# Where in a partition the MLP's stationary operands begin: two tiles allocated ahead of the weight buffers, and operand sets 32 bytes further on

## The chip, the cores and the metric

The kernel runs on one core of a Trainium2 chip. The metric is device time in microseconds (us); lower is better. Three runs of the kernel before took 2269.15, 2271.0 and 2269.58 us, median 2269.58.

## The reference

One step of a decoder layer for 320 token rows (256 prompt rows, 8 x 8 sample rows) of width 2048, in float32. Only the outline matters here:

```python
proj   = x @ w_in                                 # 2048 -> 16392 columns, split among all heads and gates
a      = mLSTM(q, k, v, gates, state)             # 4 heads, 256 x 512 matrix memory
b      = HGRN2(q, f, i, state)                    # 8 heads, 128 x 256 state
merged = sigmoid(gate_a) * (a @ w_branch_a) + sigmoid(gate_b) * (b @ w_branch_b)
x1     = layernorm(alpha * x + merged @ w_out)
hid    = square(relu(x1 @ w_up))                  # 2048 -> 8192
y      = layernorm(alpha * x1 + hid @ w_down)     # 8192 -> 2048
# y and the new states of both mixers are the outputs
```

## The kernel before

Every large product is made of float32r matmuls. A float32 operand is split into a high half (a rounded copy, made by ScalarE, ACT) and a low half (the rest, a subtraction on VectorE, DVE), and one product is the sum of three matmuls: high x high, low x high, high x low. A matmul has a stationary operand, 128 x 128, that a weight load (PEld in the profile) brings into the array, and a moving operand that streams through it. Each matmul here has its own weight load, which runs beside the matmul ahead of it. In a profile row `bank<-A,B` the names are those of the two operands in alphabetical order; with 320 columns the weights are stationary and the activations move, with 512 columns it is the other way round (below).

The phases, with their place in the profiled span:

- 0 to about 900 us: the input projection, with the two mixers' own small matmuls between. Stationary are slices of the weight halves `wh` and `wl`, moving are the 320 columns of `xh` and `xl`.
- about 900 to 1370 us: output gates, both branch projections and `w_out`, again with weights stationary (in `wh`, `wl`, and from here on in parts of `bb` as well) and 320 moving columns from `xh`, `xl`, `rxh`, `ra` and `bb`.
- about 1370 to 2236 us: the MLP, in 8 parts (`PH`) of 1024 hidden columns. The up-projection goes on with 320 moving columns. The down-projection turns the roles: stationary are 128 x 128 pieces of the hidden activations, moving are 512 columns of `w_down` (halves in `wh`, `wl` and parts of `bb`). In parts 0 to 6 a scheme with seven products in place of eight makes three kinds of units (A, B and C, of 10, 10 and 9 matmuls); part 7 is plain (kinds D and E, 16 matmuls each). The up units of the next part stand between the down units of this one.
- the last 35 us: the sample states' last outer products, the second layer norm, the outputs.

The order of all instructions is settled when the program is built, by a model of the engines; at run time each engine goes through its list and waits on semaphores.

The stationary operands of the down-projection are kept in sets, from pools that `carve_up` cuts out of the tile `xp` (which takes the place of `ra` once the mixers are done): five sets of 512 floats for B, three for A, four of 384 for S (the sample rows), one of 768 for C. The fifth S set lies in `rh`. Once `wide_parts` has run, two more sets for C and one for A come out of each of two parts of `bb`. A set holds 128-float slices side by side, each of them one stationary operand:

```python
        def part_a():
            A = X["A"] = yield acq(self.pA)
            yield from halves(two(A, 0, 128, 128), two(A, 256, 128, 128), two(flat, 0, TOK, 128), 256)
            X["a"], X["b"] = (A[:, 0:128], A[:, 256:384]), (A[:, 128:256], A[:, 384:512])
```

`down` runs the matmuls: for each pass of a unit (x0, high), (x1, high), (x0, low), or two of these for S, where x0 and x1 are the set's slices and high and low the 512 columns of `w_down`.

The tiles are allocated one after another in each partition, so the order of the lines in `__init__` and the sizes give each tile its place. In the built kernel:

| tile | first byte before | rest by 64 | rest by 512 |
|---|---|---|---|
| `xh` (rows of 1288 bytes) | 23328 | 32 | 288 |
| `wr` (raw weights) | 64544 | 32 | 32 |
| `wh` | 76832 | 32 | 32 |
| `wl` | 89120 | 32 | 32 |
| `f1`, later `bb` | 101408 | 32 | 32 |
| `rx2560`, `rx1536`, later `rxh` | 183680, 193920 | 0 | 384 |
| `ra`, later `xp` | 200064 | 0 | 384 |
| `rh` | 226688 | 0 | 384 |

All operand sets, slices and weight slices are whole multiples of 512 bytes long, so each stationary operand out of `xp` or `rh` has rest 384 by 512 (0 by 64), and each stationary or moving operand out of `wh`, `wl` or `bb` in the down-projection has rest 32.

Of the kernel before, what the change touches and what calls it, by code (L numbers as in the profile page):

```python
# [8 lines left out]
F32 = mybir.dt.float32  # L9
F32R = mybir.dt.float32r  # L10
# [164 lines left out]
class Ev:  # L175
    def __init__(self):
        self.t = None
# [199 lines left out]
class Program:  # L377
    def __init__(self, tc, nc, d, pools):
        self.nc, self.d, self.s = nc, d, Sched()
        p, ps, self.dr = pools  # L380
        self.cst = p.tile([128, C_END], F32, name="cst")
        self.lmask = p.tile([128, M_END], U8, name="lmask")
        self.vec = p.tile([128, V_END], F32, name="vec")
        self.misc = p.tile([128, 192], F32, name="misc")
        self.ones = p.tile([128, 128], F32, name="ones")
        self.xh2 = p.tile([128, KT, TOK + 2], F32R, name="xh", tag="xh")
        self.xl2 = p.tile([128, KT, TOK + 2], F32R, name="xl", tag="xl")
        self.xh, self.xl = self.xh2[:, :, 0:TOK], self.xl2[:, :, 0:TOK]
        self.RAW, self.HL = 3, 3
        self.wr = p.tile([128, self.RAW, 1024], F32, name="wr")  # L390
        self.wh = p.tile([128, self.HL, 1024], F32R, name="wh")
        self.wl = p.tile([128, self.HL, 1024], F32R, name="wl")
        self.pool = p
        self.f1 = p.tile([128, 10240], F32, name="f1", tag="f1")
        self.f2 = p.tile([128, 5204], F32, name="f2", tag="f2")
        self.f3 = p.tile([128, 5120], F32, name="f3", tag="f3")
        self.rx = [p.tile([128, n], F32, name=f"rx{n}", tag=f"rx{n}") for n in (2560, 1536)]
        self.ra = p.tile([128, 6656], F32R, name="ra", tag="ra")
        self.rh = p.tile([128, 512], F32R, name="rh")
        self.bank = [ps.tile([128, 512], F32, name=f"bank{i}") for i in range(8)]  # L400
        self.mbank = Pool(self.bank[:3])
        self.sbank = Pool(self.bank[3:])
        self.sm = Pool([self.misc[:, 32 * i:32 * i + 32] for i in range(2, 6)])
        self.lbv = self.misc[:, 0:16]
        self.eps = self.misc[:, 16:17]
        self.one = self.misc[:, 17:18]
        self.ln_b, self.exp_b = self.misc[:, 18:19], self.misc[:, 19:20]
        self.n_dma = 0
        self.ident = self.cst[:, C_ID:C_ID + 128]
# [112 lines left out]
    def carve_up(self):  # L522

        now = self.s.t["pe"]
        ra = self.Part(self.pool.tile([128, 6656], F32R, name="xp", tag="ra"))
        m3 = self.pool.tile([128, 1536], F32, name="m3", tag="rx1536")
        r2 = self.pool.tile([128, 2560], F32, name="r2", tag="rx2560")
        q = self.Part(m3)
        self.qp = [Pool([q.three(2, TOK) for _ in range(2)]), Pool([])]
        self.m_blocks = [m3[:, 512 * i:512 * i + 512] for i in range(3)] + [r2[:, 2048:2560]]  # L530
        self.raw2 = [r2[:, 0:1024], r2[:, 1024:2048]]
        self.brest = ra.ap[:, 0:2048].rearrange("p (x s v) -> p x s v", x=2, s=2)
        self.pB = Pool([ra(512) for _ in range(5)])
        self.pA = Pool([ra(512) for _ in range(3)])
        self.pS = Pool([ra(384) for _ in range(4)] + [self.rh[:, 0:384]])
        self.pC = Pool([ra(768)])
        self.zp = Pool([self.cst[:, 0:576]])
        self.st = self.cst[:, 576:576 + 72].rearrange("p (x c n) -> p x c n", x=3, c=4)
        self.mv = self.cst[:, 648:654].rearrange("p (x n) -> p x n", x=3)
        for x in self.wide_done:  # L540
            self.wide_parts(x, now)
        self.wide_done = None
# [2028 lines left out]
```

## Time and profile before

| | |
|---|---|
| median of the runs | 2269.58 us (2269.15 to 2271.0) |
| the profiled execution, its own time | 2271.41 us |
| its span, first to last instruction | 2269.6 us |
| TensorE (PE) busy | 2255.5 us (99%), 14316 matmuls |
| weight loads (PEld) busy | 2133.6 us (94%), 14316 |
| DVE busy | 1688.6 us (74%) |
| ACT busy | 1277.7 us (56%) |
| HBM traffic | 434.93 MB read, 53.53 MB written, 215 GB/s over the span |

A matmul's duration in a row runs to its modelled end, and the next one starts well before that. What a matmul costs the engine is the distance from its start to the next one's start, called the pitch below. It is read from the rows of the timeline, whose first column is the start.

### The profile page before, as it was taken

Reading aid. Unit: us, or ns where it says so; the run is one execution under the profiler, and the core shown is the slowest. Engines: PE = TensorE matmul, PEld = TensorE weight load, DVE = VectorE, ACT = ScalarE, POOL = GpSimd, SP = SyncE. Lnnn points to the kernel's source line nnn. Section 1 sums busy time; section 2 is a strip of 40 time slices with the busy share of each in tenths; the row PEclk is TensorE's granted clock in tenths of the full one; section 3 lists DMA queues with packets and bytes.
Section 4 is the critical chain, followed back from the end, with each engine's and each line's share of the span. In section 5 each row is a group of like instructions: output and inputs, shape, how many; then the busy total and the mean of one; then the engine's idle time right before and its main releaser. Section 6 shows DMA issues by size and latency. Waiting matters only on the chain.

```text
span 2269.6 us, 37822 instructions
## 1 busy us (share of the span) xinstructions
PE 2255.5 (99%) x14316; PEld 2133.6 (94%) x14316; DVE 1688.6 (74%) x2982; ACT 1277.7 (56%) x2339; POOL 12.6 (1%) x36
## 2 busy tenths in 40 slices
PE   9999999999999999999999999999999999999997
PEld 9999999999999999999999999999999999999986
DVE  5676777777777787666555769888888887888766
ACT  6566555678777766444434438565545555545442
POOL 0000000000000000000000000000000000000000
PEclk9999999999999999999999999999999999999998
DMA  7588988666666676555556545766667666767697
GB/s 283 175 263 255 275 277 248 226 185 193 183 202 203 180 217 178 172 172 172 172 173 198 195 138 174 267 243 223 238 223 243 221 228 222 245 219 240 218 259 254
DMA packets 265535, 490.95 MB, mean 216 GB/s; under 512 B 119300, under 2 KB 145540, under 8 KB 264072
## 3 DMA queue, kind: packets, MB, share of 16 engines
q1 hardware_dynamic: 260472, 482.05, 66.6%
q0 software_dynamic: 4736, 6.29, 1.1%
q8 instruction: 112, 1.84, 0.3%
q14 instruction: 71, 0.58, 0.1%
q10 hardware_dynamic: 144, 0.20, 0.0%
HBM read 434.93 MB, written 53.53 MB: 215 GB/s over the span
## 4 chain that ended last, share of the span: by engine, by line
PE 97%; ACT 1%; DMA 1%; DVE 0%; issue 0%; POOL 0%; SPq 0%; ACTq 0%
PE bank L419 97%; ACT f L413 1%; DMA bb<-vD 0%; DMA f<-first 0%; ACT wh L413 0%; ACT ra L413 0%; DVE m L2464 0%; DVE m L2463 0%; DVE wl L613 0%; SPq L422 0%; ACT m L413 0%; POOL wl L1367 0%; POOL wh L1367 0%; DVE f2m L2464 0%; DVE f2m L2463 0%
## 5 line engine op out<-in xcount | busy, mean ns | idle before, releaser
L419 PE MATMUL bank<-xh,wh 128*128 128x320 f32 (+1 forms) x2680 | 840.5, 314 | 0.2
L419 PE MATMUL bank<-xh,wl 128*128 128x320 f32 (+1 forms) x2680 | 829.0, 310 | 0.0
L419 PE MATMUL bank<-xl,wh 128*128 128x320 f32 (+1 forms) x2680 | 825.9, 309 | 0.0
L413 ACT ACTIVATE wh<-wr 128x1024 fp32r<-128x1024 f32 x430 | 452.2, 1056 | 331.4 <-PE bank L419 269.5
L613 DVE TENSOR_TENSOR wl<-wr,wh 128x1024 fp32r<-128x1024 f32 x329 | 402.7, 1224 | 294.7 <-ACT wh L413 293.8
L419 PEld LDWEIGHTS bank<-xh,wh 128*128 128x128 f32 x2680 | 503.9, 188 | 11.6 <-issue 7.3
L419 PEld LDWEIGHTS bank<-xl,wh 128*128 128x128 f32 x2680 | 503.9, 188 | 4.4
L419 PEld LDWEIGHTS bank<-xh,wl 128*128 128x128 f32 x2680 | 504.7, 188 | 0.7 <-DVE wl L971 0.3
L419 PE MATMUL bank<-xh,bb 128*128 128x320 f32 (+1 forms) x784 | 177.9, 309 | 0.0
L678 DVE TENSOR_TENSOR wl<-wr,wh 128x1024 fp32r<-128x1024 f32 x101 | 122.3, 1221 | 38.0 <-ACT wh L413 38.0
L419 PE MATMUL bank<-wh,xp 128*128 128x512 f32 x434 | 147.5, 396 | 0.0
L413 ACT ACTIVATE f<-f 32x256 f32<-32x256 f32 (+6 forms) x339 | 120.7, 357 | 36.0 <-DVE f L1575 19.0
L419 PEld LDWEIGHTS bank<-xh,bb 128*128 128x128 f32 x784 | 132.5, 188 | 1.2
L419 PE MATMUL bank<-ra,wh 128*128 128x320 f32 x468 | 128.3, 309 | 0.0
L419 PE MATMUL bank<-xl,bb 128*128 128x320 f32 (+1 forms) x392 | 121.1, 309 | 0.0
L419 PE MATMUL bank<-bb,wh 128*128 128x320 f32 (+1 forms) x524 | 116.2, 311 | 2.6 <-DMA bb<-vD 2.6
L413 ACT ACTIVATE bb<-r 128x1024 fp32r<-128x1024 f32 (+1 forms) x84 | 81.9, 983 | 61.2 <-DVE r L660 40.8
L419 PE MATMUL bank<-wl,xp 128*128 128x512 f32 x284 | 112.5, 396 | 0.0
L413 ACT ACTIVATE bb<-wr 128x512 fp32r<-128x512 f32 (+1 forms) x110 | 95.9, 884 | 21.5 <-PE bank L419 9.8
L678 DVE TENSOR_TENSOR bb<-r,bb 128x1024 fp32r<-128x1024 f32 x70 | 85.6, 1222 | 29.3 <-ACT bb L413 29.2
L419 PE MATMUL bank<-bb,xp 128*128 128x512 f32 x430 | 107.2, 396 | 0.0
L419 PEld LDWEIGHTS bank<-bb,xp 128*128 128x128 f32 x430 | 80.9, 188 | 19.4
(378 smaller groups left out, 3489.8 us busy)
## 6 DMA issues: line engine op xcount, KB each, us to landing
wr<-wt SPq DMA_DIRECT2D x432, 512.0 KB, 3.7
wr<-wd SPq DMA_DIRECT2D x108, 512.0 KB, 4.8
r<-wd SPq DMA_DIRECT2D x88, 512.0 KB, 4.6
f2m<-wd SPq DMA_DIRECT2D x44, 512.0 KB, 4.6
r<-wt SPq DMA_DIRECT2D x28, 512.0 KB, 3.5
rx<-C SPq DMA_DIRECT2D x36, 256.0 KB, 4.9
Cs<-rx SPq DMA_DIRECT2D x36, 256.0 KB, 4.5
f<-C SPq DMA_DIRECT2D x28, 256.0 KB, 4.1
```

The lines of the kernel that those rows point to most:

```text
L413: return self.nc.scalar.activation(out, in_, func, **kw)
L419: self.nc.tensor.matmul(*a, **kw)
L613: self.V().tensor_tensor(lo, raw, hi.bitcast(F32), ALU.subtract)
L678: t = yield ("dve", LO, lambda: v.tensor_tensor(lo, x, hi.bitcast(F32), ALU.subtract))
```

## The change

`ra` (later `xp`) and `rh` are allocated right behind `xl` instead of last, with a pad of 32 bytes ahead of them and another behind. In `carve_up` the first 8 floats of `xp` are skipped, so that all its operand sets, and the view `brest` that lies over them at the end, begin 32 bytes further in the tile; the S set in `rh` begins 8 floats in as well.

```diff
         self.RAW, self.HL = 3, 3
+        self.pads = [p.tile([128, 8], F32, name="pad0")]
+        self.ra = p.tile([128, 6656], F32R, name="ra", tag="ra")
+        self.rh = p.tile([128, 512], F32R, name="rh")
+        self.pads.append(p.tile([128, 8], F32, name="pad1"))
         self.wr = p.tile([128, self.RAW, 1024], F32, name="wr")
...
-        self.ra = p.tile([128, 6656], F32R, name="ra", tag="ra")
-        self.rh = p.tile([128, 512], F32R, name="rh")
...
-        self.brest = ra.ap[:, 0:2048].rearrange("p (x s v) -> p x s v", x=2, s=2)
+        ra(8)
+        self.brest = ra.ap[:, 8:2056].rearrange("p (x s v) -> p x s v", x=2, s=2)
         self.pB = Pool([ra(512) for _ in range(5)])
         self.pA = Pool([ra(512) for _ in range(3)])
-        self.pS = Pool([ra(384) for _ in range(4)] + [self.rh[:, 0:384]])
+        self.pS = Pool([ra(384) for _ in range(4)] + [self.rh[:, 8:392]])
```

No instruction is added, removed or moved: apart from line numbers, buffer numbers and addresses the program is the same, with the same waits. The places after it:

| what | first byte after | rest by 64 | rest by 512 |
|---|---|---|---|
| `xh`, `xl` | unchanged | | |
| `ra`, later `xp` | 64576 | 0 | 64 |
| first operand set in `xp` | 64608 | 32 | 96 |
| S set in `rh` | 91232 | 32 | 96 |
| `wr`, `wh`, `wl`, `f1`/`bb` | 93280, 105568, 117856, 130144 | 32 | 96 |
| `rx2560`, `rx1536` | 212416, 222656 | 0 | 448 |

The weights and everything behind them move up by 28736 bytes, 449 x 64. The stationary operands out of `xp` and `rh` go from rest 0 to rest 32 by 64; all operands of the down-projection now have the same rest by 512 among them.

## The prediction

> **What bounds the kernel now.** I read the page first, for the busiest engine and the chain of work that ended last, then who waited for whom on TensorE, then one stretch of the MLP.
>
> ```profile
> PE 2255.5 (99%) x14316; PEld 2133.6 (94%) x14316; DVE 1688.6 (74%) x2982; ACT 1277.7 (56%) x2339; POOL 12.6 (1%) x36
> ...
> PE 97%; ACT 1%; DMA 1%; DVE 0%; issue 0%; POOL 0%; SPq 0%; ACTq 0%
> ```
>
> ```profile
> PE bank L419 <- DVE m L2464: 4.2, 1, 4.2
> PE bank L419 <- DMA bb<-vD: 2.6, 1, 2.6
> PE bank L419 <- POOL ones L884: 1.0, 1, 1.0
> PE bank L419 <- DVE f3h L1883: 0.4, 1, 0.4
> ```
>
> ```profile
> 1400.00:2173.00 773.00, 773.00 (x4323) 700.89 (x4322) 650.74 (x970) 414.47 (x643) 1.86 (x2) 1.00 0.69 234
> ```
>
> TensorE carries the chain (97%) and waits 8.2 us in all, none of it between 1400 and 2173 us. There the columns are PE, PEld, DVE, ACT, POOL: PE busy throughout, DVE 651 of 773 us, the granted clock 1.00. So in the MLP the time is the number of matmuls times their pitch, and an edit that adds or removes no instruction can only move the pitch.
>
> A group's mean says nothing of the pitch, since ends are modelled and overlap; starts do. First the matmuls whose stationary operand moves, by group:
>
> ```profile
> L419 PE MATMUL bank<-wh,xp 128*128 128x512 f32 x434 | 147.5, 396 | 0.0
> ...
> L419 PE MATMUL bank<-bb,xp 128*128 128x512 f32 x430 | 107.2, 396 | 0.0
> ...
> L419 PE MATMUL bank<-wl,xp 128*128 128x512 f32 x284 | 112.5, 396 | 0.0
> ...
> L419 PE MATMUL bank<-wl,rh 128*128 128x512 f32 x34 | 13.5, 396 | 0.0
> L419 PE MATMUL bank<-wh,rh 128*128 128x512 f32 x34 | 13.4, 395 | 0.0
> L419 PE MATMUL bank<-bb,rh 128*128 128x512 f32 x28 | 7.7, 396 | 0.0
> ```
>
> That is 434 + 430 + 284 + 34 + 34 + 28 = 1244 matmuls of 512 columns. The same passes with the stationary operand in a set out of `bb`, against the same moving tiles, are the ones to set beside them. Part 7 of the MLP, one run of each (a row's xN joins matmuls that follow each other; the run ends at the next row's start):
>
> ```profile
> 2182.55 0.39 PE L419 MATMUL bank<-wh,xp 128*128 128x512 f32 x1
> ...
> 2187.93 0.87 PE L419 MATMUL bank<-bb,xp 128*128 128x512 f32 x3
> 2188.64 0.85 PE L419 MATMUL bank<-bb 128*128 128x512 f32 x3
> ...
> 2190.94 2.88 PE L419 MATMUL bank<-bb 128*128 128x512 f32 x12
> 2193.66 0.39 PE L419 MATMUL bank<-wh,rh 128*128 128x512 f32 x1
> ```
>
> From 2182.55 to 2188.64 lie 26 matmuls out of `xp`: 6.09 us, 234.2 ns each. From 2190.94 to 2193.66 lie 12 out of `bb`: 2.72 us, 226.7 ns each. A whole C unit of 9, first out of `xp`, then out of `bb`, both between 320-column matmuls:
>
> ```profile
> 1545.32 0.62 PE L419 MATMUL bank<-wh,xp 128*128 128x512 f32 x2
> ...
> 1547.42 0.31 PE L419 MATMUL bank<-xh,bb 128*128 128x320 f32 x1
> ```
>
> ```profile
> 1554.44 0.62 PE L419 MATMUL bank<-wh,bb 128*128 128x512 f32 x2
> ...
> 1556.50 0.31 PE L419 MATMUL bank<-xh,wh 128*128 128x320 f32 x1
> ```
>
> 2.10 against 2.06 us, so 233.3 against 228.9 ns. And six matmuls of an A unit out of `bb`, ahead of a B unit out of `xp`:
>
> ```profile
> 1410.63 1.53 PE L419 MATMUL bank<-bb 128*128 128x512 f32 x6
> 1412.00 0.62 PE L419 MATMUL bank<-bb,xp 128*128 128x512 f32 x2
> ```
>
> ```profile
> 1417.38 0.39 PE L419 MATMUL bank<-wl,xp 128*128 128x512 f32 x1
> 1417.61 0.31 PE L419 MATMUL bank<-xh,wh 128*128 128x320 f32 x1
> ```
>
> 1.37 us for 6, 228.3 ns; then 24 out of `xp` in 5.61 us, 233.8 ns. Everywhere the operand out of `xp` costs 4 to 8 ns more than the one out of `bb`. What differs is the place: rest 0 by 64 for the first, 32 for the second, where the moving columns have 32 in both.
>
> **The change part by part.** *The operand sets go from rest 0 to rest 32 by 64* (by 512 from 384 to the moving operand's own rest). If the place is what sets the pitch, the 1244 matmuls come to what those out of `bb` cost. In part 7 there are 16 units of 16 matmuls, 256; 8 of them take their 12 A and C matmuls from `bb`, so 256 - 96 = 160 are out of `xp` or `rh`. At 234.2 - 226.7 = 7.5 ns that is 1.2 us. The other 1084 are in parts 0 to 6. For them I take the C unit's difference, 233.3 - 228.9 = 4.4 ns, the same kind of unit between the same neighbours: 4.8 us. The bounds are none of it (the place is not the cause), and all 1244 at part 7's 7.5 ns, 9.3 us. I take 1.2 + 4.8 = 6.0 us.
>
> The trace does not show the new rest itself: both sides go to 96 by 512, where the quick rows are at 32 and 32. The nearest row is the quick one, since what the two operands have to do with each other is the same; whether 96 alone is another matter is the second rival.
>
> The Trainium skill has a rule against all this. Its page "TensorE: Matmul & The Clock Gate" (Part 2, step 4 under "Step-by-step: what each phase is for") gives TensorE two independent read ports, one for the moving operand and one for the weight load, and its page "SBUF — State Buffer" (Specifications) has lines of 16 bytes, by which a start at rest 0 and one at rest 32 are equally good. By these two the change is worth 0 us. The trace speaks against them as long as nothing but the place tells `xp` from `bb`.
>
> *The weights, `bb`, `f2`, `f3` and `rx` move by 449 x 64 bytes*, which leaves their rest by 64. The matmuls with 320 columns are the other large part of the span:
>
> ```profile
> L419 PE MATMUL bank<-ra,wh 128*128 128x320 f32 x468 | 128.3, 309 | 0.0
> L419 PE MATMUL bank<-bb,wh 128*128 128x320 f32 x512 | 112.7, 309 | 0.0
> ...
> L419 PE MATMUL bank<-xh,wl 128*128 128x320 f32 x246 | 76.1, 309 | 0.0
> ```
>
> ```profile
> 950.00:1000.00 50.00, 50.00 (x342) 1.00 0.55 171
> ...
> 1200.00:1250.00 50.00, 50.00 (x343) 1.00 0.62 201
> ```
>
> Moving from `ra` (rest 0), from `bb` (rest 32) or from `xh` (rows of 1288 bytes, so every multiple of 8) they take the same 309 ns, and a stretch of 50 us holds 342 or 343 of them, 146 ns each, whichever tile moves. So they don't mind where the moving operand begins, and I cost the move at nothing. No row shows a 320-column matmul with its stationary operand elsewhere than at rest 32, or at 96 by 512. The three largest groups alone are 8040 matmuls:
>
> ```profile
> L419 PE MATMUL bank<-xh,wh 128*128 128x320 f32 (+1 forms) x2680 | 840.5, 314 | 0.2
> L419 PE MATMUL bank<-xh,wl 128*128 128x320 f32 (+1 forms) x2680 | 829.0, 310 | 0.0
> L419 PE MATMUL bank<-xl,wh 128*128 128x320 f32 (+1 forms) x2680 | 825.9, 309 | 0.0
> ```
>
> One more or less in 343 is 0.3% of 146 ns, 0.4 ns each or 3.4 us on these; a gain or a loss below that the rows can't exclude. The far side of the loss is the second rival.
>
> *`brest` and the sets as targets.* ACT and DVE write the sets, a DMA fills `brest` once at the end. On these engines there is room (DVE 84% in the MLP), and PE waited for none of them there: nothing.
>
> *The end.* What follows the last down unit hangs on PE, so it comes earlier as a whole:
>
> ```profile
> 1379.91 847.12 PE bank L419 x4697
> ...
> 2228.83 10.17 DMA bb<-vD
> ...
> 2251.33 12.52 PE bank L419 x44
> ```
>
> In the chain PE alone stands up to 1379.91 + 847.12 = 2227.03; POOL's last transfers are released there, so the 10.17 us of transfer start earlier by what PE gains. The last 44 matmuls run in part at a lower granted clock, as the next row shows with 0.81 (the third value from the end).
>
> ```profile
> 2236.00:2270.00 34.00, 21.09 (x74) 16.50 (x72) 19.18 (x37) 8.44 (x20) 0.55 (x1) 0.81 0.66 231
> ```
>
> Where the slow stretches fall can shift by some of the 12.5 us' share: I allow 2 us to either side and cost it at nothing.
>
> **The sum.** The profiled execution took 2271.41 us with a span of 2269.6, that is 1.8 us over the median of the runs. 2271.41 - 6.0 = 2265.4 for it; for the median 2269.58 - 6.0 = 2263.6 us.
>
> **Rivals.** *First, the place is not the cause.* `xp` is written all through the MLP, the sets in `bb` too, but `xp` also lay above byte 200000, and the trace holds no quick operand from there nor a slow one below. If it is something else that goes with the tile, nothing changes: 2269.6 us. The two pages of the Trainium skill named above speak for this case. In the rows, what speaks for it is that none shows one tile at both places; what speaks against it is that `rh`, a tile of its own, has the same 395 to 396 ns rows as `xp`, and that the bb operands between 117792 and 134176 are all quick. If the high addresses were the cause the move would cure it as well, so that case gives 2263.6 too.
>
> *Second, slower: the weights' new rest by 512 is bad for weight loads.* The 8040 matmuls above, and the smaller groups of 320 columns, load their weights out of `wh`, `wl` and `bb`, now at 96 instead of 32. The misplaced stationary operand costs the 512-column matmul 4.4 to 7.5 ns; in the share of 320/512 that would be 2.8 to 4.7 ns, 22 to 38 us on 8040, and the gain would fall away too, since `xp` goes to the same rest: 2292 to 2308 us. It decides the sign from 6.0 us / 8040 = 0.75 ns a matmul on. Against it: only the rest by 64 told quick from slow so far, and that stays.
>
> *Third, PE gains and loses it again*: DVE, at 651 of 773 us, has the next least room. An MLP shorter by 6 us makes that 651 of 767, 85%; the low halves of the raw weights come from it. A wait for it could give back half: 2266.6 us. Against it: no wait there now.
>
> **How the numbers follow.** The forecast (place sets the pitch, PE passes it on) has 0.73, with a range of its own from 9.3 us plus something at the end to 4 us: 2259.5 to 2266. The first rival has 0.13, the second 0.07, the third 0.07. No change can be told within 0.2%, 4.5 us. Faster by more than that are the forecast down to 2265.0 (0.66) and little of the third (0.02), 0.68; slower is the second, 0.07; the rest, 0.25, is within. To leave out no more than 2 in 10 the range reaches from 2260 over the forecast's and the third's cases into the first rival's: 2269.7.
>
> **What would show it.** In the changed profile the run of 26 in part 7 takes 5.9 us instead of 6.09, a C unit out of `xp` 2.06 instead of 2.10, and the whole `xp` groups have means near those of `bb`. The matmul count in 50 us of the branch projections stays at 342 or 343. No new PE wait in the MLP; POOL's last transfer issued some 6 us earlier. I am wrong if the `xp` runs keep 234 ns, if the 320-column stretches hold 341 or fewer, or if a wait for DVE stands in the MLP.

## The result, and the profile after

The changed kernel takes 2262.84 us (median of 7 runs, 2259.1 to 2264.3) against 2269.83 for the kernel before (7 runs, 2269.15 to 2271.05): 7.0 us less, a ratio of 0.9966 with a 95% interval of 0.9954 to 0.9977. 2263.6 was forecast. The profiled execution took 2264.3 us, its span is 2262.5.

The page of the changed kernel, busy times and chain:

```profile
PE 2247.8 (99%) x14316; PEld 2135.7 (94%) x14316; DVE 1687.1 (75%) x2982; ACT 1277.1 (56%) x2339; POOL 12.6 (1%) x36
...
PE 97%; ACT 1%; issue 1%; DMA 0%; DVE 0%; POOL 0%; POOLq 0%; ACTq 0%
```

TensorE has the same 14316 matmuls and still carries the chain; it is busy 7.7 us less. Whom it waited for (total, times, longest):

```profile
PE bank L421 <- DMA xp<-vD: 4.2, 1, 4.2
PE bank L421 <- DMA bb<-vD: 3.4, 1, 3.4
PE bank L421 <- POOL ones L887: 1.0, 1, 1.0
PE bank L421 <- DVE f3h L1886: 0.3, 1, 0.3
```

8.9 us instead of 8.2, all but 0.3 at the two ends of the span; the MLP still has no wait. The groups with the stationary operand out of `xp` or `rh`:

```profile
L421 PE MATMUL bank<-wh,xp 128*128 128x512 f32 x434 | 144.7, 390 | 0.0
...
L421 PE MATMUL bank<-wl,xp 128*128 128x512 f32 x284 | 110.6, 389 | 0.0
...
L421 PE MATMUL bank<-bb,xp 128*128 128x512 f32 x430 | 104.0, 389 | 0.0
...
L421 PE MATMUL bank<-wh,rh 128*128 128x512 f32 x34 | 13.2, 389 | 0.0
```

389 to 390 ns where it was 395 to 396: every group fell alike. The timeline gives the pitch, start to start. The run of 26 out of `xp` in part 7, then a run of 12 out of `bb`:

```profile
2175.78 0.39 PE L421 MATMUL bank<-wh,xp 128*128 128x512 f32 x1
...
2181.68 0.62 PE L421 MATMUL bank<-bb 128*128 128x512 f32 x2
```

```profile
2183.94 2.88 PE L421 MATMUL bank<-bb 128*128 128x512 f32 x12
2186.66 0.39 PE L421 MATMUL bank<-wh,rh 128*128 128x512 f32 x1
```

5.90 us for 26 is 226.9 ns (before 234.2); 2.72 us for 12 is 226.7 (before the same). And the C unit of 9 out of `xp`:

```profile
1544.75 0.63 PE L421 MATMUL bank<-wh,xp 128*128 128x512 f32 x2
...
1546.80 0.30 PE L421 MATMUL bank<-xh,bb 128*128 128x320 f32 x1
```

2.05 us, 227.8 ns a matmul by these rounded rows and 228.6 by the unrounded starts (before 2.10 us). Over all starts in the two traces (pitches above 300 ns, at the end of the span, left out) the mean pitch of the 1244 matmuls went from 233.94 to 226.99 ns, that is 8.6 us; the `bb` sets' went from 228.8 to 227.7. Together that is 9.3 us, and the span shows 7.1 of it. Of the rest, 1.2 us are lost ahead of the MLP: its first 512-column matmul starts later than before. First the row of the kernel before, then that of the changed one:

```profile
1403.61 0.63 PE L419 MATMUL bank<-wh,xp 128*128 128x512 f32 x2
```

```profile
1404.76 0.40 PE L421 MATMUL bank<-wh,xp 128*128 128x512 f32 x1
```

The end came along with PE, as expected: POOL's last transfers into `wh` and `wl` begin at 2219.5 instead of 2227.1, and the last 44 matmuls at 2244.30 instead of 2251.33, 24.8 us behind them instead of 24.3. So the stretch from the first of these rows to POOL's transfers is 814.8 us instead of 823.5, 8.7 less, and 8.7 - 1.2 - 0.4 for the end is the 7.1. From the chain of the changed kernel:

```profile
2219.54 0.84 POOL wh L1370
...
2237.01 7.16 DMA xp<-vD
2244.17 0.14 issue
2244.30 12.43 PE bank L421 x44
```

### The profile page after: what moved, and what is told of

Read it like the earlier page. It is cut to its first block, busy times and chain, and to the rows that moved or that the text cites. A ratio compares the mean times of both kernels' runs of the same rounds, so it can differ in the third digit from the quotient of the medians.

```text
span 2262.5 us, 37822 instructions
## 1 busy us (share of the span) xinstructions
PE 2247.8 (99%) x14316; PEld 2135.7 (94%) x14316; DVE 1687.1 (75%) x2982; ACT 1277.1 (56%) x2339; POOL 12.6 (1%) x36
## 4 chain that ended last, share of the span: by engine, by line
PE 97%; ACT 1%; issue 1%; DMA 0%; DVE 0%; POOL 0%; POOLq 0%; ACTq 0%
PE bank L421 97%; ACT f L415 1%; DMA xp<-vD 0%; ACT wh L415 0%; ACT ra L415 0%; DVE wl L616 0%; POOL wl L1370 0%; POOL wh L1370 0%; POOL bb L1373 0%; ACT f3h L415 0%; ACT rh L415 0%; PE bank L1101 0%; DVE f L1766 0%; DVE f L1578 0%; DVE f3h L1886 0%
```

## The experiments

"Distance" below is the stationary operand's first byte less the moving operand's, by 256. The kernel before has 96 (352 by 512), the changed one 0. The theories: the stationary operand's own rest by 64 sets the pitch ("own-rest"), or the agreement of the two operands in it ("agreement"), both readings of the prediction; agreement by a larger number; the tiles' new place. Where a pitch is called slow or quick, slow is a mean of about 232 ns or more and quick one of about 227.

### The skip alone

```diff
-        self.brest = ra.ap[:, 0:2048]...
+        ra(8)
+        self.brest = ra.ap[:, 8:2056]...
-        ... [self.rh[:, 0:384]])
+        ... [self.rh[:, 8:392]])
```

> The kernel before with the 8 skipped floats alone: no tile is reallocated, no pad; xp and rh stay above byte 200000 and their sets go from rest 0 to rest 32 by 64 (416 by 512, where the moving operands have 32). If the rest by 64 sets the pitch (agreement of the two operands, or the stationary operand's own), runs out of xp fall from 234 to about 227 ns and the time to 2260 to 2262 us. If the high address was the cause: 234 ns and 2269.8 us. If the two operands have to agree by 512: 234 ns and 2269.8 us. If the 1 us that the span lost before the MLP comes from the moved weights, it is not lost here (matmul 9200 at 1334.4 us and not 1335.3).

Measured: 2268.69 us against 2270.31, ratio 0.9991 (0.9982 to 1.0). The part 7 run in its timeline:

```profile
2180.11 0.40 PE L419 MATMUL bank<-wh,xp 128*128 128x512 f32 x1
...
2186.16 0.62 PE L419 MATMUL bank<-bb 128*128 128x512 f32 x2
```

6.05 us for 26, 232.7 ns. The two operands agree by 64 here, by 128 too (distance 128), and the run is still slow. So the rest by 64 is not the cause, neither the operand's own nor agreement in it. Matmul 9200 starts at 1333.99 us: nothing is lost ahead of the MLP here.

### The new place alone

The changed kernel without the skip (sets at distance 224, that is 32 bytes short of agreement):

> The changed kernel without the skip: ra, rh and the pads stand where the change puts them, but the sets begin at the tile's start, rest 0 by 64 (64 by 512), against moving operands at 32 (96 by 512). Rest by 64: runs out of xp stay at 234 ns, time 2269.8 us, or 2270.8 with the 1 us before the MLP. High address as the cause: 227 ns and 2261 to 2263 us.

Measured: 2270.86 us, ratio 1.0002 (0.9993 to 1.0011).

```profile
2182.07 0.39 PE L421 MATMUL bank<-wh,xp 128*128 128x512 f32 x1
...
2188.14 0.62 PE L421 MATMUL bank<-bb 128*128 128x512 f32 x2
```

6.07 us, 233.5 ns. The place alone does nothing; each half of the change alone gives next to nothing, and the two together 7 us.

### Moving the weights instead

```diff
+        self.pads = [p.tile([128, 8], F32, name="pad0")]
         self.wr = p.tile([128, self.RAW, 1024], F32, name="wr")
```

> The kernel before with one pad of 32 bytes ahead of the raw weights and nothing else, so that everything behind it swaps its rest by 64: weights, bb and its sets go from 32 to 0, xp and rh from 0 to 32. Agreement theory: xp against the weights still disagrees, 234 ns, the bb sets agree, 227 to 229 ns, time 2269.8 us. Own-rest theory (a stationary operand at 32 is quick, at 0 slow): xp quick at 227, the bb sets slow at 234; 1244 x 7 ns gained and 645 x 5 ns lost, 2264 us, if the 320-column matmuls, whose stationary weights now lie at rest 0, don't mind; if they do by the share of 320/512, 4 ns on 8040 and more, 2296 us or above.

Measured: 2272.24 us, ratio 1.0007 (0.9998 to 1.0016). All rests by 64 are swapped, the distance stays 96, and so does the pitch: 2184.48 to 2190.57 us for 26, 234.2 ns.

```profile
2184.48 0.39 PE L420 MATMUL bank<-wh,xp 128*128 128x512 f32 x1
...
2190.57 0.62 PE L420 MATMUL bank<-bb 128*128 128x512 f32 x2
```

The 320-column matmuls with their weights at rest 0 reach the MLP at 1403.99 us, the kernel before at 1403.61: far from the 32 us that 4 ns on 8040 matmuls would cost, so the second rival's mechanism is out at that size. They do mind a little: the 2688 of 320 columns from the MLP's start on take 395.4 us by their starts and 394.2 in the kernel before. That is 1.2 us, and 0.5 more are lost ahead of the MLP (see "The two quick versions").

### Weights, `bb`, `xp` and `rh` all at rest 0 by 64

A second pad of 8 floats, ahead of `f3`; the distance is 128, as with the skip alone.

> As the one before with a second pad of 32 bytes ahead of f3, so that xp and rh are back at rest 0 by 64 while the weights and bb are at 0 too (64 by 512 against 448). Agreement theory: all 512-column matmuls are quick, 227 ns, time 2260 to 2262 us. Own-rest theory: all are slow, 234 ns, 2269.8 + 645 x 5 ns = 2273 us. If the operands have to agree by 512: xp 234 ns, 2269.8 us.

Measured: 2270.91 us, ratio 1.0 (0.9991 to 1.0009).

```profile
2182.78 0.40 PE L421 MATMUL bank<-wh,xp 128*128 128x512 f32 x1
...
2188.83 0.62 PE L421 MATMUL bank<-bb 128*128 128x512 f32 x2
```

6.05 us, 232.7 ns: at other addresses and the other rest by 64, the same pitch as the skip alone, which has the same distance. The two runs agree matmul by matmul: the 26 pitches lie between 228 and 241 ns, and each is the same in both traces. The kernel before and the one with the single pad, both at distance 96, also agree in each of their 26 pitches, to within 1 ns. So at these two distances the pitch goes with the distance, and the addresses don't count.

### Agreement without moving a tile

The kernel before with 40 floats skipped in `xp` and in `rh`: 384 + 160 is 544, rest 32 by 512, where the weights are.

```diff
+        ra(40)
+        self.brest = ra.ap[:, 40:2088]...
+        ... [self.rh[:, 40:424]])
```

> The kernel before with 40 floats skipped ahead of the sets in xp and 40 in rh, and nothing else: the tiles stay where they were, xp above byte 200000, and the sets' rest by 512 becomes 32, that of the moving operands (distance 0), with the stationary operands at rest 32 by 64 as in the variant with 8 floats skipped. If the distance by 512 sets the pitch: 226.7 ns in the runs out of xp, 2261 to 2263 us, as the change or better. If it takes the new place of the tiles as well as the rest (the change's two parts together): 232 to 234 ns and 2268 to 2270 us.

Measured: 2260.14 us against 2270.22, ratio 0.9957 (0.9945 to 0.997).

```profile
2173.48 0.39 PE L419 MATMUL bank<-wh,xp 128*128 128x512 f32 x1
...
2179.38 0.62 PE L419 MATMUL bank<-bb 128*128 128x512 f32 x2
```

226.9 ns from tiles that stay above byte 200000. The whole of the gain is here, from an edit of three lines: the new place is not needed.

### How close an agreement

Four variants of the changed kernel with 72, 24, 12 and 9 floats skipped instead of 8: 256, 64, 16 and 4 bytes more.

> The changed kernel with 72 floats skipped instead of 8: stationary operands 256 bytes from the moving ones' rest by 512. If only agreement by 512 is quick: 232 to 234 ns, 2268 to 2271 us. If agreement by 256 is enough: 226.7 ns and 2262 to 2263 us. If the new place of the tiles is what counts: 226.7 ns.

Measured: 2262.47 us, ratio 0.9965 (0.9952 to 0.9979). Agreement by 256 is enough:

```profile
2175.51 0.39 PE L421 MATMUL bank<-wh,xp 128*128 128x512 f32 x1
...
2181.40 0.61 PE L421 MATMUL bank<-bb 128*128 128x512 f32 x2
```

> The changed kernel with 24 floats skipped instead of 8: 64 bytes apart by 512, the same rest by 64. Agreement by 512: 232 to 234 ns, 2268 to 2271 us. Agreement by 64 together with the new place: 226.7 ns, 2262 to 2263 us.

Measured: 2271.22 us, ratio 1.0005 (0.9996 to 1.0014). The run goes from 2182.99 to 2189.05 us, 233.1 ns: the same rest by 64 and the new place, and all of the gain gone.

```profile
2182.99 0.40 PE L421 MATMUL bank<-wh,xp 128*128 128x512 f32 x1
...
2189.05 0.62 PE L421 MATMUL bank<-bb 128*128 128x512 f32 x2
```

> The changed kernel with 12 floats skipped instead of 8: 16 bytes apart by 512. If the two have to agree exactly: 232 to 234 ns, 2268 to 2271 us. If a small distance costs in proportion (16 of 32 bytes of the 233.2 ns that 32 bytes gave): about 230 ns, 2266 us.

Measured: 2265.28 us, ratio 0.9973 (0.9962 to 0.9984), between the two, but not in proportion. In the timeline a run of 29 out of `xp` that follows 320-column matmuls, then one of 53 that follows six matmuls out of `bb`:

```profile
1421.14 0.63 PE L421 MATMUL bank<-wh,xp 128*128 128x512 f32 x2
...
1427.91 0.31 PE L421 MATMUL bank<-xh,wh 128*128 128x320 f32 x1
```

```profile
1470.78 0.84 PE L421 MATMUL bank<-bb,xp 128*128 128x512 f32 x3
...
1482.79 0.30 PE L421 MATMUL bank<-xh,wh 128*128 128x320 f32 x1
```

6.77 us for 29 is 233.4 ns; 12.01 for 53 is 226.6. At this distance a run keeps one pitch to its end, with hardly a value between. Of the 24 runs that follow 320-column matmuls 23 are slow (232.5 to 234.0 ns) and one, the first, is quick. Of the 32 that follow other 512-column matmuls 29 are quick, and three of 3 or 4 matmuls have 230 to 231. The mean of 228.8 ns is a mixture.

> The changed kernel with 9 floats skipped instead of 8: stationary and moving operands 4 bytes apart by 256. At 16 bytes apart the runs that follow a quick run stayed at 226.7 ns and those that follow 320-column matmuls kept 233 to 234 to their end. If any distance does that: the same split, mean 228.8 ns, 2265 us. If 4 bytes, within one 16-byte piece, count as agreement: 226.7 to 227 ns throughout, 2262 to 2263 us.

Measured: 2271.32 us, ratio 1.0004 (0.9995 to 1.0014). Both expectations failed: 4 bytes apart, runs are slow throughout, 2182.94 to 2188.97 us for the 26, 231.9 ns.

```profile
2182.94 0.39 PE L421 MATMUL bank<-wh,xp 128*128 128x512 f32 x1
...
2188.97 0.63 PE L421 MATMUL bank<-bb 128*128 128x512 f32 x2
```

So nearness does not count, and 16 bytes are better than 4. All distances tried, with the mean pitch of the matmuls out of `xp` and `rh` over all their starts:

| distance by 256, bytes | kernels | mean pitch, ns | median, us |
|---|---|---|---|
| 0 | the change; 40 skipped; 72 skipped | 226.99; 227.06; 226.99 | 2262.84; 2260.14; 2262.47 |
| 4 | 9 skipped | 232.85 | 2271.32 |
| 16 | 12 skipped | 228.8, two kinds of runs | 2265.28 |
| 64 | 24 skipped | 233.4 | 2271.22 |
| 96 | before; one pad | 233.9; 234.0 | 2269.83; 2272.24 |
| 128 | skip alone; two pads | 232.5; 232.7 | 2268.69; 2270.91 |
| 224 | new place alone | 233.2 | 2270.86 |

### The two quick versions side by side

> The variant with 40 floats skipped and no tile moved, once more, on one chip with the changed kernel. If moving the weights by 28736 bytes costs the 320-column matmuls something (the six profiles with moved weights reach matmul 9200 at 1334.5 to 1335.3 us, the three without at 1333.5 to 1334.4): about 1 us less than the changed kernel, 2261 against 2262 us. If not: the same time.

> The changed kernel itself, on one chip with the variant above: 2262 to 2263 us against about 2270 for the kernel before.

Measured on one chip: 2261.92 us (2257.86 to 2263.59; ratio 0.9962, 0.995 to 0.9975) without moved tiles, 2261.44 (2259.23 to 2262.8; ratio 0.9964, 0.9951 to 0.9976) for the changed kernel. The times don't tell them apart, but the traces do. The seven profiles of kernels whose weights moved by 28736 bytes have their first 512-column matmul of the MLP at 1403.93 to 1405.13 us, the four of kernels that don't move them at 1402.78 to 1403.73. The first 100 matmuls alone differ by up to 0.9 us, within each group and between two executions of one kernel. From matmul 100 to that first 512-column matmul the four without moved weights take 1385.65 to 1385.69 us, five of the seven with moved weights 1386.37 to 1386.40, 0.7 more. The changed kernel's own two profiles take 1386.66 and 1387.76; they hold besides, at 364 us, a delay of 0.3 and 1.3 us that the others don't have. In the MLP the 320-column matmuls take 393.9 to 394.2 us without and 394.4 to 394.9 with moved weights, 0.6 more by the mean. So moving the weights costs about 1.3 us, and this is no accident of one execution.

Where it comes from can be seen in the single pitches. From 33 to 68 us the input projection repeats 48 matmuls five times (16 rows of `xh` and `xl`, three matmuls a row). Each of the 48 has its own pitch, 141 to 154 ns, the same to about 1 ns in every repetition and in all four profiles without moved weights. The rows lie 1288 bytes apart, 8 more than a multiple of 256, so weights that begin 32 bytes later meet at any row the distance that they had four rows (12 matmuls) earlier. And there the pitches reappear. Nine in a row of the kernel before, from 40.49 us, are 143, 146, 150, 141, 147, 147, 150, 147 and 153 ns. With the single pad of 32 bytes the same nine places have 143, 147, 145, 145, 145, 153, 145, 145 and 146; but 12 matmuls later, from 42.07 us, stand 143, 147, 149, 141, 147, 147, 151, 146 and 154. Of all 48 mean pitches 38 reappear 12 matmuls later to within 2 ns (the first four rows set against the last four), and 17 at the same place. So the 320-column matmuls go by the distance as well; over the 16 rows it nearly averages out, and the average changes by 0.1 ns, from 146.4 to 146.5 ahead of the MLP.

## Why the prediction was right, and where it was not

- **What bounds.** Right: PE without a wait in the MLP, so time is count times pitch. It passed on what it gained; DVE stayed at 649.7 us in a stretch of 765, and no wait for it came (the third rival did not happen):

```profile
1400.00:2165.00 765.00, 765.00 (x4322) 700.82 (x4321) 649.69 (x969) 414.83 (x646) 1.03 (x1) 1.00 0.70 236
```

- **The place of the operands sets the pitch.** Right as a mechanism, and the first rival (the place is not the cause) is out: 40 skipped floats bring all of it. But the prediction read it as the rest by 64, "rest 0 by 64 for the first, 32 for the second", and this step failed. The kernel with the skip alone has that rest and gains 1.6 us. What counts is the distance between stationary and moving operand by 256. The prediction has it in brackets ("by 512 from 384 to the moving operand's own rest") and falls back on it for the new rest ("what the two operands have to do with each other is the same"), but its cause and its second rival ("only the rest by 64 told quick from slow so far") go by 64, though the rest by 512 told them apart as well. The change has distance 0 because its two parts together add up to it; by the rest by 64 the skip alone would have been forecast to do as well, and that is wrong. As far as the forecast went by 64, that it came true is luck.
- **The size.** 6.0 us was the sum, 8.6 us is what the 1244 matmuls gave. The term that was too small is the 4.4 ns for the 1084 of parts 0 to 6, taken from C units out of `bb`. For the C units themselves that was about right (233.2 to 228.6 ns by the starts of the unit shown above). But their 9 matmuls pay for what stands around them: over all 34 such units out of `bb` in the trace of before, the first five matmuls behind 320-column ones average 230.7 ns and the other four 226.7. Only 8 such units, 72 matmuls, come out of `xp`. Longer runs out of `xp` settle at the 226.7 ns of part 7, so the upper bound's price held nearly everywhere. The count of part 7 was off too: by the rows 136 of its 256 matmuls are out of `xp` or `rh`, not 160; that changes the sum by less than 0.1 us. The `bb` sets gained 0.7 us besides, probably since their neighbours became quick.
- **The weights' move costs nothing.** Wrong by about 1.3 us, which lies below the 3.4 us that the prediction's rows could exclude. "So they don't mind where the moving operand begins" came from group means and counts in 50 us; the single pitches do depend on it. Of the 9.3 us, 1.2 are missing ahead of the MLP (0.7 from the move, 0.3 from the one delay at 364 us, 0.2 from the first 100 matmuls), 0.4 went into the MLP's 320-column matmuls and 0.4 into the end; 0.2 can't be placed. A gain put too small and losses left out partly cancel, so the forecast time is nearer than its terms.
- **The second rival**, bad weight loads at rest 96, did not happen at the size that it named (22 to 38 us): a stretch from 950 to 1000 us holds 342 matmuls as before. What the move does cost is the 1.3 us above.

```profile
950.00:1000.00 50.00, 50.00 (x342) 50.00 (x341) 30.09 (x47) 21.13 (x27) 0.00 (x0) 1.00 0.55 173
```

- **The rule on ports.** The Trainium skill's page "TensorE: Matmul & The Clock Gate" (Part 2, "Step-by-step: what each phase is for") has independent read ports for the two operands. Read as "it does not matter where the two begin", which is how the prediction put it against the change, that does not hold here: with nothing but their distance changed, the pitch of the 512-column matmuls goes from 226.7 to 233 ns. What makes them depend on each other, the ports or something else, no run shows.

## What to carry to other kernels

Where a kernel is bound by matmuls that each load their own weights, compare the pitch (start to start) of the same matmul from different tiles before looking for waits; a duration of 396 against 389 ns hides a difference of 7 in 234. If it differs by tile, write down the operands' first bytes by 256, and shift a set by a few floats until stationary and moving operands agree; here that took neither a pad nor a new order of tiles. Shown are 512-column float32r matmuls of one kernel; other shapes are to be measured. Test the rule on a kernel that has only one reading of it: here two rests agreed at once in the quick rows, and the variant with the skip alone told them apart. And look at single pitches, not at group means alone: the means hid that the 320-column matmuls depend on the distance too.

## What the runs showed of the hardware that was not expected

- 512-column float32r matmuls, each with a 128-column weight load, follow each other in 226.7 ns when the two operands agree by 256 bytes, and in 232 to 234 ns on average at five other distances (4, 64, 96, 128 and 224). Distances 0, 96 and 128 were met at two or more sets of addresses, with the same pitch each time. Within a slow run the single pitches go from 227 to 241 ns in a series that repeats.
- 320-column ones, with moving rows at every multiple of 8 bytes, take mostly 141 to 154 ns each, by the distance at their row, and 146.4 to 147.1 on average in all kernels.
- At a distance of 16 bytes there are two lasting states: 233.4 ns for 29 matmuls on end and 226.6 ns for 53, nearly always by what ran ahead.
- What waits (the next weight load or the moving columns), and why the distance matters by 256, stays open; no run here separates them.
